# A two-layer hybrid decoder trunk: raw weight tiles in the common pool, the first weight ahead of x, low parts on DVE and token 0 ending alone

## The chip, the cores and the metric

The kernel runs on one core of a Trainium2 chip. The metric is the device time of one execution in microseconds (us); lower is better. The engines are PE (TensorE, matrix multiplication), DVE (VectorE), ACT (ScalarE), POOL (GpSimd) and SP (SyncE, which here only issues transfers).

## The reference

The input is `x`, 512 tokens by 1024 features, float32. Two layers follow one another; layer 0 mixes tokens by sliding-window attention, layer 1 by a chunked spatial gating unit (SGU):

```
for i in range(2):
    x += rmsnorm(mixer_i(rmsnorm(x)))        # mixer 0: attention, mixer 1: SGU
    x += rmsnorm(swiglu(rmsnorm(x)))         # the FFN, 2816 hidden features

attention: 16 query heads, 4 key/value heads of 64, rotary positions, window 128,
           a learned sink per head; softmax over 256 keys for each block of 128 queries
SGU:       z = gelu(h @ w_in); u, v = halves of z
           y = u * (tril(w_s) @ layernorm(v) + b_s); out = y @ w_out
swiglu:    (silu(h @ w_gate) * (h @ w_up)) @ w_down
```

All of it is float32.

## The kernel before, in words

Every float32 product is made of three matmuls. A tile is split into a high part (`hh` of activations, `wh` of weights) in a shorter type that PE multiplies at full rate, and the remainder (`hl`, `wl`); the product is high × high + high × low + low × high (`mm3`), summed in PSUM (`acc` tiles of 128 × 512). All of these matmuls have one line in the profile, L272.

Weights stream once through the core: 240 blocks of 128 × 1024 (512 KB), each a `raw` tile brought by a transfer issued on SP (L303). A block, or the sum of two for the FFN's product scheme, becomes one chunk: ACT writes the high part (`split`, L344), then DVE, or POOL for the first two chunks (`POOL_LOW`), subtracts it from raw to give the low part (L325 on DVE, L322 on POOL). `raw` tiles lie in a pool of their own of `NRAW` = 4, the split tiles, the tiles `xg` and the row constants in a pool `wp` of `NW` = 15. A transfer for a raw tile is issued when its slot is free; SP issues in the program's order.

The order of instructions on PE, DVE and ACT is the order in which Python emits them, and a planner sets it while it does. The main line emits matmuls and advances a clock of its own (`now`). Everything beside it (evacuations, norms, splits) is a `Side`, a generator with a due time; `tick()` runs whatever has come due between two matmuls, and when nothing is due, `split_idle()` may emit the next split, if two slots of `wp` are free. `until(f)` and `wait(t)` let time pass; as long as `now` is under `WARM`, they fill it with matmuls on a tile of zeros (`pass_time`, L240).

Stages follow in this order: projections q, k, v and attention (0 to about 180 us in the trace), the first FFN (to 548), the SGU, the second FFN. In attention a query block's probabilities are scaled (L1079 on DVE, L1083 on ACT), transposed by PE (`aux`, L1116), evacuated by ACT (`t`, L1120) and multiplied by v (PV, L1108: `acc<-t,vt`, four for a head pair). ACT and DVE then split the result into `ga` (L1130 high, L1135 low) for the output projection (`acc<-wh,ga`). The rotary step copies on ACT (L966, L976).

At the end of an FFN each token block (four of 128 tokens) has two halves of 512 features, which are 18 matmuls each; `ends` says in which order they are made. DVE adds a finished half to the block's sum `m` (L901), ACT sums squares (L476), DVE scales by the norm's row (L604), takes the reciprocal root in a chain of small steps on 128 × 1 values (L482 to L471, `rsqrt`), updates `x` (L617), and normalised x is transposed by PE (L554), from which `hh` (ACT, L567) and `hl` (DVE, L571) of the next stage come. The last token block of the second FFN ends in two quarters (L930) and the output x (L662).

At the start the tiles `xg` (x transposed, four tiles of 512 KB) become `hh` and `hl` with the norm's scales `c_cols` (L1390, L1393); `ORDER` says how these tiles and the first weight blocks follow one another on SP. Meanwhile `x` itself is read for the row sums of squares, whose reciprocal roots reach the query tiles through a small matmul (L1431).

Of the kernel before, what the change touches and what calls it, by code (L numbers as in the profile page):

```python
# [23 lines left out]
MAGIC = 0x5F3759DF  # L24
NW = 15
NP = 2
# [3 lines left out]
NT = 3  # L30
NRAW = 4
SETS = (8, 8)
# [5 lines left out]
DLAT = 1.7  # L38
X_0 = 4.0
RS = (0.27406385, -4.2420223, 5.2654107, -0.90349173, 1.7067959)  # L40
# [3 lines left out]
DIAG = (0, 1)  # L44
POOL_LOW = (0, 1)
ALT = (1, 2, 3)
WARM = 5.5
ORDER = (0, "w", 1, 2, "w", 3)
ACT_SQ = ()
# [100 lines left out]
def trunk_kernel(ctx, tc, x_t, xt, w, cols, rows, ws_t, consts, out):  # L150
# [6 lines left out]
    gp = pool("gp", 2)  # L157
    rawp = pool("rawp", NRAW)
    wp = pool("wp", NW)
# [7 lines left out]
    def nm(s):  # L167
        cnt[0] += 1
        return f"{s}_{cnt[0]}"
# [65 lines left out]
    def pass_time(t):  # L235
        if now[0] < WARM:
            if idle_ps[0] is None:
                idle_ps[0] = acc()
            while now[0] + 0.12 < min(t, WARM):
                nc.tensor.matmul(idle_ps[0][:, 0:256], zero[:, 0:P], zero[:], start=True, stop=True)  # L240
                now[0] += 0.214 if now[0] < 4.0 else 0.107
        now[0] = max(now[0], t)
# [42 lines left out]
    raws, chunks = {}, {}  # L285
    used, cur, hold, pace = [0], [0], [0.0], [5.1]
    left = [CB * u for _, _, u in STREAM]
    raw_used = [0]

    def fetch(free=0.0, most=NBLK):  # L290
        while len(raws) < min(NCH, most) and raw_used[0] + len(STREAM[len(raws)][0]) <= NRAW:
            c = len(raws)
            if c == NLATE:
                load_x()
# [6 lines left out]
            for b in reversed(STREAM[c][0]):  # L301
                raw = rawp.tile([P, CB * P], F32, tag="raw", name=nm("raw"))
                nc.sync.dma_start(raw[:], w[b])  # L303
                busy["d"] = max(busy["d"], now[0], free) + 1.46
                tiles.insert(0, raw)
# [3 lines left out]
    def split():  # L309
        c = len(chunks)  # L310
        fetch()
        tiles, ready = raws[c]
        raw = tiles[0]
        assert used[0] + 2 <= NW
        used[0] += 2
# [33 lines left out]
    def split_idle():  # L349
        c = len(chunks)  # L350
        if c >= NCH or used[0] + 2 + spare[0] > NW or (c and not chunks[c - 1][2].done):
            return False
# [9 lines left out]

    spare, stage = [0], [0]

    def chunk(i):
        c = i // CB
        while c >= len(chunks):
            until(lambda: not chunks or chunks[len(chunks) - 1][2].done)
            split()
        return c, chunks[c]  # L370
# [18 lines left out]

    def row_tile(o):  # L390
        used[0] += 1
        assert used[0] <= NW
        t = wp.tile([P, D], F32, tag="w", name=nm("row"))
        nc.sync.dma_start(t[:], rows[272 + o * D:272 + (o + 1) * D].partition_broadcast(P))
        return t
# [20 lines left out]
    xg = [wp.tile([P, 2, S], F32, tag="w", name=f"xg{q}") for q in range(NB)]  # L416
    used[0] += NB
    nc.gpsimd.dma_start(c_id[:], consts[:, 1280:1408])
    nc.gpsimd.dma_start(c_cols[:], cols)
    nc.gpsimd.dma_start(c_row[:], rows[0:272].partition_broadcast(P))  # L420
# [283 lines left out]
    def ffn(base, nx_in, g1o, nx_out):  # L704
# [188 lines left out]
        if 1:  # L893
            spare[0] = 0
            g1 = row_tile(g1o)
# [7 lines left out]

            ends = [(0, 0), (0, 1), (1, 0), (1, 1)]
            if nx_out is None:
                ends.pop()
            ends = [((0, 1), 0), ((0, 1), 1)] + [((2 + i,), c) for i, c in ends]
            for n, (ts, c) in enumerate(ends):
                if n == 2:
                    hold[0] = now[0] + 4 * BJ * 0.65  # L910
                for t in ts:
# [635 lines left out]
```

## Time and profile before

| what | value |
|---|---|
| runs | 1058.65, 1058.82, 1059.26 us; median 1058.82 |
| the profiled execution | 1059.33 us, of which the profile's span is 1057.5 |
| mean granted clock of PE | 0.989 |
| busy | PE 1031.1, weight load 854.7, DVE 684.7, ACT 469.6, POOL 23.8 us |
| matmuls | 5126 |
| moved from HBM | 135.69 MB, 130 GB/s over the span |

A row of the timeline is: start, duration, engine, line, operation, output <- inputs, size, count, and in brackets the engine's idle time before it and what ended that. A row of waits is: engine, what it was about to make, who ended the wait, us in total, how often, the longest. Span and run differ by what lies around the program.

### The profile page before, as it was taken

What the parts mean: (1) busy time and instruction counts of PE and PEld (TensorE: products, weight loads), DVE (VectorE), ACT (ScalarE), POOL (GpSimd) and SP (SyncE); (2) the same over time, 40 slices, a digit from 0 to 9 for tenths busy, and PEclk for the clock granted to TensorE, in tenths of its full rate; (3) what the DMA queues carried; (4) which work ended last, traced back from release to release, by engine and by line L of the source; (5) the groups of instructions that cost most, each with busy time, mean ns of one, the idle gap of its engine ahead of it and who ended that gap; (6) DMA issues with size and microseconds to landing.
All of it is one profiled execution on the core that took longest, in us unless ns stands there. A gap on an engine that the chain in (4) does not pass through costs nothing.

```text
span 1057.5 us, 13471 instructions
## 1 busy us (share of the span) xinstructions
PE 1031.1 (97%) x5126; PEld 854.7 (81%) x5126; DVE 684.7 (65%) x1276; ACT 469.6 (44%) x817; POOL 23.8 (2%) x22
## 2 busy tenths in 40 slices
PE   8998998999999999999989999999999999999996
PEld 7875665998888888888878888899888888888885
DVE  6798678743446566778495777474245666687736
ACT  5798666542233343435265343464224333334411
POOL 2000002000000000000010000010000000000000
PEclk9998999999999999999999999999999999999999
DMA  9422011343425644655431333133344553565402
GB/s 334 138 82 80 21 60 41 100 127 113 139 82 178 199 122 157 222 188 191 156 116 60 104 103 121 56 121 120 120 140 131 178 174 124 188 203 193 163 21 80
DMA packets 39057, 138.66 MB, mean 131 GB/s; under 512 B 4368, under 2 KB 4896, under 8 KB 38992
## 3 DMA queue, kind: packets, MB, share of 16 engines
q1 hardware_dynamic: 38304, 136.66, 39.3%
q8 instruction: 40, 0.66, 0.3%
q10 hardware_dynamic: 576, 0.92, 0.2%
q0 software_dynamic: 112, 0.23, 0.2%
q14 instruction: 25, 0.20, 0.1%
HBM read 135.69 MB, written 2.10 MB: 130 GB/s over the span
## 4 chain that ended last, share of the span: by engine, by line
PE 92%; DVE 3%; ACT 2%; issue 1%; DMA 0%; POOL 0%; DVEq 0%; ACTq 0%; POOLq 0%
PE acc L272 89%; PE acc L1108 1%; PE aux L1116 1%; PE aux L554 1%; ACT p L1070 1%; DMA c_cols<-cols 0%; ACT rt L966 0%; DVE wl L325 0%; DVE x L617 0%; DVE hl L1393 0%; ACT wh L344 0%; PE aux L552 0%; ACT t L1120 0%; DVE m L1210 0%; DVE rc L471 0%
## 5 line engine op out<-in xcount | busy, mean ns | idle before, releaser
L272 PE MATMUL acc<-hh,wh 128*128 128x512 f32 (+1 forms) x960 | 352.1, 367 | 0.0
L272 PE MATMUL acc<-hl,wh 128*128 128x512 f32 (+1 forms) x960 | 349.9, 364 | 0.0
L272 PE MATMUL acc<-hh,wl 128*128 128x512 f32 (+1 forms) x960 | 349.7, 364 | 0.0
L325 DVE TENSOR_TENSOR wl<-raw,wh 128x1024 fp32r<-128x1024 f32 x198 | 241.9, 1230 | 151.1 <-PE acc L272 78.2
L272 PEld LDWEIGHTS acc<-hh,wh 128*128 128x128 f32 x960 | 181.1, 189 | 29.4 <-issue 0.2
L272 PEld LDWEIGHTS acc<-hh,wl 128*128 128x128 f32 x960 | 181.1, 189 | 28.7
L272 PEld LDWEIGHTS acc<-hl,wh 128*128 128x128 f32 x960 | 181.1, 189 | 28.6 <-issue 0.2
L344 ACT ACTIVATE wh<-raw 128x1024 fp32r<-128x1024 f32 x160 | 165.6, 1052 | 55.0 <-PE acc L272 48.3
L272 PE MATMUL acc<-wh,rt 128*128 128x512 f32 x496 | 162.3, 389 | 0.0
L272 PE MATMUL acc<-wh,ga 128*128 128x512 f32 (+1 forms) x344 | 120.3, 399 | 3.6 <-DVE ga L1135 2.9
L272 PEld LDWEIGHTS acc<-wh,rt 128*128 128x128 f32 x496 | 93.1, 188 | 19.4
L272 PE MATMUL acc<-wl,rt 128*128 128x512 f32 x248 | 96.5, 389 | 0.0
L272 PEld LDWEIGHTS acc<-wh,ga 128*128 128x128 f32 x344 | 65.2, 191 | 21.1 <-DVE ga L1135 3.8
L853 DVE TENSOR_TENSOR m<-m,acc 128x512 f32<-128x512 f32 x80 | 51.8, 684 | 44.2 <-PE acc L272 33.0
L272 PE MATMUL acc<-wl,ga 128*128 128x512 f32 (+1 forms) x206 | 80.0, 388 | 0.0
L332 ACT ACTIVATE wh<-raw 128x1024 fp32r<-128x1024 f32 x40 | 42.3, 1059 | 71.0 <-DVE raw L337 71.0
L831 ACT ACTIVATE rt<-t 128x512 fp32r<-128x512 f32 x40 | 25.3, 633 | 87.1 <-DVE t L826 68.7
L740 ACT ACTIVATE t<-acc 128x512 f32<-128x512 f32 (+1 forms) x38 | 20.1, 529 | 95.0 <-PE acc L272 95.0
L272 PEld LDWEIGHTS acc<-wl,rt 128*128 128x128 f32 x248 | 46.6, 188 | 9.6
L337 DVE TENSOR_TENSOR raw<-raw,raw 128x1024 f32<-128x1024 f32 x40 | 48.8, 1219 | 0.0
L272 PEld LDWEIGHTS acc<-wl,ga 128*128 128x128 f32 x206 | 39.3, 191 | 6.6
L598 POOL TENSOR_TENSOR m<-m,row 128x512 f32<-128x512 f32 x12 | 16.8, 1407 | 1012.1 <-ACT acc L476 1012.1
(135 smaller groups left out, 990.5 us busy)
## 6 DMA issues: line engine op xcount, KB each, us to landing
raw<-w SPq DMA_DIRECT2D x240, 512.0 KB, 3.6
row<-rows SPq DMA_DIRECT2D x8, 512.0 KB, 5.2
xg<-xt SPq DMA_DIRECT2D x4, 512.0 KB, 7.1
x<-x_t SPq DMA_DIRECT2D x4, 512.0 KB, 11.9
out<-x SPq DMA_DIRECT2D x4, 256.0 KB, 2.1
out<-x ACTq DMA_DIRECT2D x3, 256.0 KB, 2.1
cs<-consts SPq DMA_DIRECT2D x1, 512.0 KB, 8.3
t<-ws_t SPq DMA_DIRECT2D x2, 256.0 KB, 5.9
```

Of the source, the lines that this page charges most:

```text
L272: nc.tensor.matmul(ps, a, b, start=start, stop=stop)
L325: nc.vector.tensor_tensor(wl[:], raw[:], wh[:].bitcast(F32), ALU.subtract)
L332: nc.scalar.activation(wh[:], raw[:], AF.Copy)
L337: nc.vector.tensor_tensor(raw[:], raw[:], tiles[1][:], op)
L344: nc.scalar.activation(wh[:], raw[:], AF.Copy)
L554: nc.tensor.transpose(dst, self.src[t][k // 4][:, (k % 4) * P:(k % 4 + 1) * P], ident)
L598: nc.gpsimd.tensor_tensor(self.m[c][:], self.m[c][:], self.g1[:, cols2[c]], ALU.mult)
L740: nc.scalar.activation(t1[:, hf], pg[:, hf], AF.Silu)
L831: nc.scalar.activation(hi, src, AF.Copy)
L853: nc.vector.tensor_tensor(d, d, ps[i][:], ALU.subtract if sign == "-" else ALU.add)
L1070: nc.scalar.activation(p(j), p(j), AF.Exp, bias=st[:, j:j + 1], accum_out=sm[:, j:j + 1])
L1108: nc.tensor.matmul(po[i * 64:i * 64 + 64, :], vt[n - nkt + 1 + kt][:, o:o + 64], todo[2 * kt + i], start=kt == 0, stop=kt == nkt - 1)
```

## The change

- `rawp` is gone. Raw tiles come from `wp`, which grows from 15 to 19 tiles; the planner counts `used + raw_used` against `NW`. At most 2 raw tiles may be outstanding, and 4 in stages 2 and 6, the gate and up products of the FFNs (`NRAW`). `room()` asks for a fetched block and two free slots before a split, and a row constant's tile waits for a slot.
- `ORDER`: the first weight block is fetched ahead of the first `xg`.
- `c_cols` is fetched by the first instruction of ACT's queue, not of POOL's; ACT runs a small activation on zeros right after it (`first_act`).
- `POOL_LOW` is empty: the first two low parts are made by DVE.
- `WARM` goes from 5.5 to 8.0, and a matmul on zeros counts 0.214 throughout: 37 instead of 26 of them.
- `ends`: of tokens 0 and 1 only the first halves are made together; token 0's second half now precedes token 1's. `hold` grows from 4 to 5 units.
- `X_0`, the planner's time for the first x tile, goes from 4.0 to 4.9.

```diff
-NW = 15
+NW = 19
-NRAW = 4
+NRAW = (2, 4)
-X_0 = 4.0
+X_0 = 4.9
-POOL_LOW = (0, 1)
+POOL_LOW = ()
-WARM = 5.5
-ORDER = (0, "w", 1, 2, "w", 3)
+WARM = 8.0
+ORDER = ("w", 0, 1, 2, "w", 3)
...
-    rawp = pool("rawp", NRAW)
...
-                now[0] += 0.214 if now[0] < 4.0 else 0.107
+                now[0] += 0.214
...
     def fetch(free=0.0, most=NBLK):
-        while len(raws) < min(NCH, most) and raw_used[0] + len(STREAM[len(raws)][0]) <= NRAW:
+        while len(raws) < min(NCH, most):
             c = len(raws)
+            n = len(STREAM[c][0])
+            if raw_used[0] + n > NRAW[stage[0] in (2, 6)] or used[0] + raw_used[0] + n > NW:
+                return
...
-                raw = rawp.tile([P, CB * P], F32, tag="raw", name=nm("raw"))
+                raw = wp.tile([P, CB * P], F32, tag="w", name=nm("raw"))
...
     def split():
         c = len(chunks)
-        fetch()
...
-        if c >= NCH or used[0] + 2 + spare[0] > NW or (c and not chunks[c - 1][2].done):
+        if c >= NCH or used[0] + raw_used[0] + 2 > NW or (c and not chunks[c - 1][2].done):
...
+    def room():
+        fetch()
+        return len(chunks) in raws and used[0] + raw_used[0] + 2 <= NW
 
     def chunk(i):
         c = i // CB
         while c >= len(chunks):
-            until(lambda: not chunks or chunks[len(chunks) - 1][2].done)
-            split()
+            until(lambda: c < len(chunks) or (not chunks or chunks[len(chunks) - 1][2].done) and room())
+            if c >= len(chunks):
+                split()
         return c, chunks[c]
...
     def row_tile(o):
+        until(lambda: used[0] + raw_used[0] < NW)
         used[0] += 1
...
+    nc.scalar.dma_start(c_cols[:], cols)
+    first_act = sp.tile([P, 8], F32, tag="first", name="first", bufs=1)
+    nc.vector.memset(first_act[:], 0.0)
+    nc.scalar.activation(first_act[:], first_act[:], AF.Copy)
     nc.gpsimd.dma_start(c_id[:], consts[:, 1280:1408])
-    nc.gpsimd.dma_start(c_cols[:], cols)
...
-            ends = [(0, 0), (0, 1), (1, 0), (1, 1)]
+            ends = [((0, 1), 0), ((0,), 1), ((1,), 1), ((2,), 0), ((2,), 1), ((3,), 0), ((3,), 1)]
             if nx_out is None:
                 ends.pop()
-            ends = [((0, 1), 0), ((0, 1), 1)] + [((2 + i,), c) for i, c in ends]
             for n, (ts, c) in enumerate(ends):
                 if n == 2:
-                    hold[0] = now[0] + 4 * BJ * 0.65
+                    hold[0] = now[0] + 5 * BJ * 0.65
```

Because the planner decides with these numbers, the order of instructions changes beyond the lines of the diff. Three places follow; the numbers behind an underscore tell tiles apart, and lines of the changed kernel stand a few higher than before.

On ACT at the program's start, before (`wh_183` is the first weight block, `hh` are the high parts of x):

```order
L1390 ACT_TABLE_LOAD
L1390 ACTIVATE hh_125<-xg_99,c_cols 128x512
L1390 ACTIVATE hh_126<-xg_99,c_cols 128x512
L344 ACTIVATE wh_183<-raw_107 128x1024
L1390 ACTIVATE hh_127<-xg_100,c_cols 128x512
L1390 ACTIVATE hh_128<-xg_100,c_cols 128x512
```

and now (L424 is the transfer of the scales, L427 the small activation, L346 the split, L1397 the high parts of x):

```order
L424 DMA c_cols<-cols 128x42
L427 ACT_TABLE_LOAD
L427 ACTIVATE first<-first 128x8
L346 ACTIVATE wh_169<-raw_106 128x1024
L1397 ACTIVATE hh_125<-xg_96,c_cols 128x512
L1397 ACTIVATE hh_126<-xg_96,c_cols 128x512
L1397 ACTIVATE hh_127<-xg_97,c_cols 128x512
```

The table load, the scales' transfer and the weight's high part have moved ahead of the first `hh`.

On ACT in the attention, about 148 to 153 us in the trace before (`t_1592` is the last of four transposed tiles that PE's PV needs, L476 a sum of squares, L344 a weight's split):

```order
L1120 ACTIVATE t_1572<-aux_1567 128x512
L1083 ACTIVATE p_1461<-p_1461,sm_1460 128x256
L1067 ACTIVATE es_1459<-es_1459 128x4
L1070 ACTIVATE p_1461,sm_1460<-p_1461,st_1458 128x256 x4
L476 ACTIVATE acc_1500,sq_1499<-m_1011 128x512
L344 ACTIVATE wh_1584<-raw_997 128x1024
L1120 ACTIVATE t_1592<-aux_1587 128x512
```

and now (`t_1591` is that tile, L485 the sum of squares):

```order
L1127 ACTIVATE t_1571<-aux_1566 128x512
L1090 ACTIVATE p_1468<-p_1468,sm_1467 128x256
L1074 ACTIVATE es_1466<-es_1466 128x4
L1077 ACTIVATE p_1468,sm_1467<-p_1468,st_1465 128x256 x4
L1127 ACTIVATE t_1591<-aux_1586 128x512
L485 ACTIVATE acc_1507,sq_1506<-m_966 128x512
L346 ACTIVATE wh_1598<-raw_1283 128x1024
```

The fourth `t` has moved ahead of the sum of squares and of the split. On PE, six matmuls of the output projection stand between the first two and the last two PV matmuls there, where before those four stood together with only a transpose between.

On DVE near the end of the attention, about 178 to 183 us (`ga_118` is the low part of the last attention output, L617 the update of x, L1210 an add to the output sum):

```order
L617 SCALAR_TENSOR_TENSOR x_91<-m_1013,rc_1826,x_91 128x512
L617 SCALAR_TENSOR_TENSOR x_91<-m_1014,rc_1826,x_91 128x512
L325 TENSOR_TENSOR wl_1838<-raw_1276,wh_1837 128x1024
L1210 TENSOR_TENSOR m_1016<-acc_1804,m_1016 128x512
L1135 TENSOR_TENSOR ga_118<-acc_1782,ga_117 128x4x128
```

and now:

```order
L626 SCALAR_TENSOR_TENSOR x_88<-m_968,rc_1849,x_88 128x512
L626 SCALAR_TENSOR_TENSOR x_88<-m_969,rc_1849,x_88 128x512
L327 TENSOR_TENSOR wl_1829<-raw_1643,wh_1828 128x1024
L1142 TENSOR_TENSOR ga_118<-acc_1781,ga_117 128x4x128
L1217 TENSOR_TENSOR m_971<-acc_1832,m_971 128x512
```

`ga_118` has moved ahead of the add; on PE six matmuls that do not need it now stand between the last PV and its first use, where before there was none.

At the end of the first FFN, on PE, the transposes of tokens 0 and 1 came before six matmuls of token 3's last half and the first of the next stage; now 18 matmuls of token 3's last half stand between the third group of transposes and the first matmul of the next stage.

More of the change, by code (lines that the diff above doesn't have):

```diff
@@ L286, in trunk_kernel @@
     used, cur, hold, pace = [0], [0], [0.0], [5.1]
+    stage = [0]
     left = [CB * u for _, _, u in STREAM]
@@ L310, in split @@
         c = len(chunks)
-        fetch()
         tiles, ready = raws[c]
         raw = tiles[0]
-        assert used[0] + 2 <= NW
+        assert used[0] + raw_used[0] + 2 <= NW
         used[0] += 2
@@ L361, in split_idle @@
         return True
-    spare, stage = [0], [0]
+    def room():
+        fetch()
+        return len(chunks) in raws and used[0] + raw_used[0] + 2 <= NW
     def chunk(i):
@@ L390, in row_tile @@
     def row_tile(o):
+        until(lambda: used[0] + raw_used[0] < NW)
         used[0] += 1
-        assert used[0] <= NW
         t = wp.tile([P, D], F32, tag="w", name=nm("row"))
@@ L893, in ffn @@
         if 1:
-            spare[0] = 0
             g1 = row_tile(g1o)
```

## The prediction

> **What bounds the kernel now.** I read the busy shares first, then the list of TensorE's (PE's) waits, then the granted clock around those waits.
>
> ```profile
> span 1057.5 us, 13471 instructions
> PE 1031.1 (97%) x5126; PEld 854.7 (81%) x5126; DVE 684.7 (65%) x1276; ACT 469.6 (44%) x817; POOL 23.8 (2%) x22
> ```
>
> ```profile
> PE acc L1108 <- ACT t L1120: 6.6, 3, 3.8
> PE acc L272 <- ACT wh L344: 3.1, 1, 3.1
> PE acc L272 <- DVE ga L1135: 2.9, 2, 2.6
> PE acc L272 <- DVE hl L571: 2.7, 1, 2.7
> ...
> PE acc L272 <- DVE hl L1393: 0.8, 1, 0.8
> PE acc L272 <- ACT ga L1130: 0.7, 1, 0.7
> ```
>
> PE is idle for 1057.5 − 1031.1 = 26.4 us. The six waits (us in total, times, longest) hold 16.8 of them; most of the rest is the tail after the last matmul. Since the matmuls stay as they are, the change can win only idle PE time and time at a lower clock:
>
> ```profile
> 9.00:13.00 4.00, 3.47 (x17) 3.47 (x18) 3.23 (x3) 3.88 (x6) 2.42 (x2) 0.57 1.03 420
> 98.00:106.00 8.00, 6.51 (x29) 4.04 (x30) 4.91 (x15) 4.34 (x9) 0.00 (x0) 0.57 0.22 66
> 152.00:157.00 5.00, 5.00 (x26) 3.70 (x25) 3.82 (x13) 1.34 (x3) 0.00 (x0) 0.66 0.32 105
> 182.00:188.00 6.00, 5.11 (x20) 4.20 (x21) 5.81 (x29) 1.71 (x4) 1.28 (x1) 0.72 0.30 94
> 551.00:557.00 6.00, 5.93 (x20) 4.64 (x21) 5.91 (x10) 1.78 (x3) 0.00 (x0) 0.72 0.79 251
> 557.00:1049.00 492.00, 492.00 (x2440) 418.34 (x2440) 302.98 (x505) 191.47 (x289) 8.48 (x6) 1.00 0.39 126
> ```
>
> Columns: stretch, its length, busy time of PE, weight load, DVE, ACT and POOL, then the granted clock (third number from the right). The last row is the steady state: PE full, clock 1.00, nothing to win. After each long wait the clock is lower: (1 − 0.66) × 5 = 1.7 us of PE time lost at 152, and likewise 1.7 at 182 and 1.7 at 551, 1.7 at 9 and 3.4 at 98 (of which 0.7 falls into the wait itself, so 2.7). So a wait of 2.6 us costs about 4.3.
>
> **The start** (one term for ORDER, c_cols, the early activation, POOL_LOW and WARM).
>
> ```profile
> 1.06 5.39 PE L240 MATMUL acc<-zero 128*128 128x256 bf16 x26 [1.06 <-DVE zero L232]
> 1.94 5.24 DMA c_cols<-cols
> 4.84 1.28 ACT L1390 ACT_TABLE_LOAD   x1 [4.84 <-DMA xg<-xt]
> 7.20 1.33 ACT L1390 ACTIVATE hh<-xg,c_cols 128x512 fp32r<-128x512 f32 x2 [1.07 <-DMA c_cols<-cols]
> 9.53 0.58 PE L272 MATMUL acc<-wh,hh 128*128 128x256 f32 x1 [3.08 <-ACT wh L344]
> 12.96 2.45 POOL L322 TENSOR_TENSOR wl<-raw,wh 128x1024 fp32r<-128x1024 f32 x1 [1.02 <-ACT wh L344]
> 13.04 1.34 ACT L1390 ACTIVATE hh<-xg,c_cols 128x512 fp32r<-128x512 f32 x2 [0.16 <-DMA xg<-xt]
> 13.07 2.89 DVE hl L1393
> 16.01 0.39 PE L272 MATMUL acc<-wh,hl 128*128 128x256 f32 x1 [0.84 <-DVE hl L1393]
> 19.83 0.88 PE L272 MATMUL acc<-wl,hh 128*128 128x256 f32 x6
> L325 DVE TENSOR_TENSOR wl<-raw,wh 128x1024 fp32r<-128x1024 f32 x198 | 241.9, 1230 | 151.1 <-PE acc L272 78.2
> ```
>
> Before, c_cols holds the first hh until 7.2, the first weight follows on ACT, and PE starts at 9.53 with the clock gone. Then the low part hl of the third x tile takes 2.89 us while POOL runs a low part beside it; 31 more matmuls of 0.12 us lead from 16.01 to the low pass near 19.7. After: with the first weight ahead of xg, the first xg lands one 512 KB transfer after 4.84 (some 1.3 us, so 6.1), ACT has split the weight by then, and its table is loaded before any data is there. PE starts at about 7 to 7.6, when the warm-ups end: at 5.39 / 26 = 0.207 us the 37 of them would reach 8.7, somewhat less once the clock rises; a start as late as 8.7 still does not bind, because the fourth xg, which stays the sixth transfer, does. Its hh starts at 13.04 and takes 1.34. DVE, without POOL beside it, has one new low part of 1.23 before the first hl and one before the fourth pair; hl at 0.7 each follows hh at 0.7 distance: 13.04 + 1.34 + 0.7 ≈ 15.2. The last eight matmuls follow, so the low pass starts at about 16.3: gain 3.4. Bounds: 2 (if DVE stretches again by about 1.4) and 4. What hides the two low parts (2.5 us of DVE) is its wait for hh; if that cover is gone, hl is late by up to 1.2, inside the bound. The row statistics end at 23.9 as before and are next needed after 18 instead of 15 matmuls of the first query tile, at about 24.1 by the new clock: this just fits.
>
> **The attention stalls** (a consequence of the shared pool, its planner conditions and NW: splits are issued earlier or later, and with them the order on ACT and DVE).
>
> ```profile
> 60.00:98.00 38.00, 35.42 (x196) 25.20 (x194) 36.56 (x107) 36.65 (x86) 0.00 (x0) 1.00 0.25 84
> 95.51 2.91 ACT L966 ACTIVATE rt<-rt,c_cols 32x512 f32<-32x512 f32 x4
> 99.49 1.97 PE L1108 MATMUL acc<-t,vt 128*64 128x512 f32 x2 [3.78 <-ACT t L1120]
> 149.61 0.58 ACT L476 ACTIVATE acc<-m 128x512 f32<-128x512 f32 x1
> ...
> 150.22 1.04 ACT L344 ACTIVATE wh<-raw 128x1024 fp32r<-128x1024 f32 x1
> ...
> 151.80 1.07 PE L1108 MATMUL acc<-t,vt 128*64 128x512 f32 x2 [2.58 <-ACT t L1120]
> ...
> 180.42 1.21 DVE L325 TENSOR_TENSOR wl<-raw,wh 128x1024 fp32r<-128x1024 f32 x1
> 182.89 0.76 PE L272 MATMUL acc<-wh,ga 128*128 128x512 f32 x2 [2.60 <-DVE ga L1135]
> ```
>
> At 99.49 ACT itself is full (36.65 of 38 us): between two evacuations t it runs 5.2 us before and 4.4 us in the new order (2.91 of rotary copies, 0.95 weight, 0.54 copy). The stall shrinks from 3.78 to about 3.2 and the lower clock most likely stays: gain 0.5 (−2 to 4, the upper end if the clock holds).
>
> At 151.80 the awaited t stood behind a row sum (0.61) and a weight split (0.95); now it stands ahead of both, and six output matmuls (1.4 us) lie between the first two and the last two probability matmuls. 2.58 − 0.61 − 0.95 − 1.4 is below zero; I leave 0.6 for the matmuls that are missing as cover where they stood, and 0.7 for three transposes now in a row: gain 2.58 + 1.7 − 1.3 = 3.0 (0 to 4.3).
>
> At 182.89 the awaited ga stood behind two x updates, a weight's low part and an add; now it stands ahead of the add (0.6), and six matmuls (1.4) follow the last probability matmul. The chain that remains, split 0.95, low part 1.21 and ga 0.6, is 2.8 from the probability matmuls' start, and PE has 0.9 + 1.4 + 0.5 = 2.8 of work: a remainder of about 1 with both waits there, and the clock stays up. Gain 0.69 + 2.60 + 1.7 − 1.0 = 4.0, of which I take 3.5.
>
> A row that speaks against counting all this: the granted clock falls at 98, 152.7, 183.4 and 552, some time after a wait begins and even with work running. The Trainium skill, "TensorE: Matmul & The Clock Gate", Part 1, says that activity is judged in a free-running window of about 3.4 us and the clock halves after an idle one. Taken strictly, waits of 2.6 us would cost no clock, and the sum would be 5.1 smaller; the trace disagrees, since 1.7 us of clock were lost after each. That the windows run freely agrees: what is left of a wait can fall whole into one window or be shared between two.
>
> **The seam from the first FFN to the gating unit, and the tail** (ends and hold).
>
> ```profile
> 546.18 0.14 DVE L482 SCALAR_TENSOR_TENSOR u<-sq 128x1 f32<-128x1 f32 x1
> ...
> 547.47 1.41 DVE L617 SCALAR_TENSOR_TENSOR x<-m,rc,x 128x512 f32<-128x512 f32 x2
> 548.80 0.68 DVE L901 TENSOR_TENSOR m<-acc,m 128x512 f32<-128x512 f32 x1
> ...
> 550.54 0.87 DVE L571 SCALAR_TENSOR_TENSOR hl<-aux,c_cols,hh 128x256 fp32r<-128x256 f32 x2
> ...
> 551.07 0.50 PE L272 MATMUL acc<-wh,hl 128*128 128x512 f32 x1 [2.68 <-DVE hl L571]
> ...
> 1050.08 0.75 DVE L930 TENSOR_TENSOR m<-acc,m 128x256 f32<-128x256 f32 x2
> ```
>
> Before, tokens 0 and 1 end together, and 2.68 us of PE time go by until their second hl pair, behind x update, add and weight on DVE. Now token 0 ends a half (18 matmuls of 0.23 = 4.1 us) earlier. From the end of token 2's first half DVE needs add 0.7, hl 0.9, the small chain 1.3 (546.18 to 547.47), x 1.4, weight 1.2, add 0.7, hl 0.9 = 7.1, while PE has 42 matmuls and four transpose groups (9.6 + 1.4 = 11.0); at the third pair it is 11.9 against 13.7. So nothing is late: gain 2.68 + 1.7 = 4.4 (2 to 4.4; the third pair is next, by 1.8). In the tail x of token 2 and the add of the last token's first quarter are done before PE's last matmul (1049.6), not after it: DVE starts the last add at 1049.65, ACT's square follows, and the small chain starts at about 1050.8, while before two adds and two scalings (0.75 a pair) from 1050.08 on put it near 1051.7: gain 0.9 (0.3 to 1.3).
>
> **The shared raw tiles themselves.** Weight transfers now wait for slots that PE frees, and they are issued in order on SP. By the program's order each transfer's slot is free at least 13 us of PE time before its first use, and 24 in the FFNs. From issue to use it needs its landing plus 1.0 (ACT) plus 1.2 (DVE), so I cost it at nothing:
>
> ```profile
> raw<-w SPq DMA_DIRECT2D x240, 512.0 KB, 3.6
> ```
>
> **Sum.** 3.4 + 0.5 + 3.0 + 3.5 + 4.4 + 0.9 = 15.7. The order is new throughout the attention, where ACT and DVE are nearly full, so I give one new short wait with its lost clock back, 1.7. The profiled execution took 1059.33 (span plus 1.83; 0.5 above the median, 1058.82): 1059.33 − 14.0 = 1045.3.
>
> **Rivals.**
> 1. The attention stalls form again elsewhere: 96% of ACT in that stretch leaves no room, and only the order moves. Against it: the waits at 152 and 183 stand behind single instructions that have moved. Then start, seam and tail remain, 3.4 + 4.4 + 0.9 = 8.7, and one more stall of 2.6 + 1.7 may take half of that back: 1050.6 to 1055.
> 2. Slower: raw tiles in the shared pool. Outside the gate and up stages two transfers may be outstanding, and SP issues in order, so one that waits for PE holds those behind it. A use takes 1057 / 240 = 4.4 us a block and the way from slot to weight 3.6 + 1.0 + 1.2 = 5.8: a transfer let go only one block ahead stalls PE by 1.4, with 1.7 of clock each time 3.1. Five such blocks undo the gain, seven give 1067. The leads of 13 us speak against it.
> 3. The stalls fall across two windows: the clock holds at 99 too, 2.7 more: 1042.6. The Trainium skill, "TensorE: Matmul & The Clock Gate", Part 1, would have it so for a wait under 3.4 us.
> 4. The change does little: the low parts on DVE delay hl as POOL did, and the seam's chain is late at its third pair: start 1, tail 0.9, and the attention as in rival 1: about 1057.5, within what a measurement of this kernel can tell from no change, 0.2% or 2.1 us.
>
> **How the numbers follow.** Forecast (1044 to 1050) 0.61, rival 1 0.18, rival 2 0.09, rival 3 0.07, rival 4 0.05. Leaving out rival 2, rival 4 and a piece of rival 1 gives 1041.5 to 1055. Faster by over 0.2% holds the forecast, rivals 1 and 3: 0.86; same 0.05; slower 0.09.
>
> **What would show it.** PE's first real matmul before 8.8, the low pass at 16 to 17, clock 1.00 through 9 to 13; no wait over 1.5 us and clock 1.00 near 148 and 180; a wait of about 3 us still near 95; no wait at the seam near 535 to 550; the small chain within 1.3 us of the last matmul. Wrong would be: new waits of PE on L344's or L325's successors with a raw transfer behind them (rival 2), or waits on t and ga of 2 us or more at other places (rival 1).

## The result and the profile after

The changed kernel takes 1044.27 us (median of 4 runs, 1044.11 to 1044.54) against 1059.04 for the kernel before in the same session (1058.65 to 1059.56): the ratio is 0.986, 95% interval 0.9843 to 0.9878. 1045.3 was forecast, 1041.5 to 1055. The profiled execution took 1044.54, its span is 1042.8.

The head of the profile after, and its list of PE's waits:

```profile
span 1042.8 us, 13516 instructions
PE 1026.1 (98%) x5137; PEld 851.5 (82%) x5137; DVE 683.0 (65%) x1279; ACT 470.9 (45%) x818; POOL 18.5 (2%) x19
```

```profile
PE acc L1115 <- ACT t L1127: 3.9, 1, 3.9
PE acc L271 <- DVE ga L1142: 3.9, 2, 2.7
...
PE acc L271 <- DVE hl L1400: 0.4, 1, 0.4
...
```

PE's idle time falls from 26.4 to 1042.8 − 1026.1 = 16.7 us. Its busy time falls by 5.0 although there are 11 more matmuls on zeros; this is the clock. Two waits of over 2 us are left. Neither is near 148, where the wait at 152 stood before (first row), nor at the seam (second row). The columns are those of the prediction, PE's busy time first and the clock third from the right:

```profile
144.00:152.00 8.00, 7.75 (x52) 4.42 (x53) 4.87 (x18) 7.48 (x22) 0.00 (x0) 1.00 0.00 0
530.00:548.00 18.00, 18.00 (x89) 14.93 (x88) 16.29 (x41) 14.36 (x30) 1.29 (x1) 1.00 0.57 205
```

Since most matmuls keep their place in PE's order, the start of the same matmul in both traces tells where the time went. This table is worked out from the timelines' PE rows:

| place | before | after | lead | gained since the row above |
|---|---|---|---|---|
| first weight's low pass (`wl,hh`) | 19.83 | 16.91 | 2.92 | 2.9 |
| before the second half of the attention | 137.45 | 134.97 | 2.48 | −0.4 |
| between the places of the waits at 152 and 183 | 167.18 | 160.80 | 6.37 | 3.9 |
| in the first FFN | 199.43 | 190.31 | 9.12 | 2.7 |
| in the SGU | 576.39 | 562.59 | 13.80 | 4.7 |
| last matmul | 1049.30 | 1035.57 | 13.73 | −0.1 |
| end of the span | 1057.5 | 1042.8 | 14.7 | 1.0 |

The rows of the timeline after that stand behind it, in order of time:

```profile
7.89 0.36 PE L271 MATMUL acc<-wh,hh 128*128 128x256 f32 x1
10.92 0.39 PE L271 MATMUL acc<-wh,hl 128*128 128x256 f32 x1 [0.40 <-DVE hl L1400]
11.86 1.06 ACT L346 ACTIVATE wh<-raw 128x1024 fp32r<-128x1024 f32 x1
12.97 0.39 PE L271 MATMUL acc<-wh,hh 128*128 128x256 f32 x1
14.09 1.41 DVE L1400 SCALAR_TENSOR_TENSOR hl<-xg,c_cols,hh 128x512 fp32r<-128x512 f32 x2
16.91 4.00 PE L271 MATMUL acc<-wl,hh 128*128 128x256 f32 x32
...
86.41 0.51 PE L271 MATMUL acc<-wh,ga 128*128 128x512 f32 x1 [1.21 <-DVE ga L1142]
...
97.08 1.97 PE L1115 MATMUL acc<-t,vt 128*64 128x512 f32 x2 [3.95 <-ACT t L1127]
...
149.75 0.66 PE L1123 MATMUL aux<-c_id,p 128*128 128x128 f32 x4 [0.25 <-ACT t L1127]
...
173.79 0.89 PE L271 MATMUL acc<-wh,ga 128*128 128x512 f32 x2 [2.67 <-DVE ga L1142]
...
1036.94 0.16 DVE L491 SCALAR_TENSOR_TENSOR u<-sq 128x1 f32<-128x1 f32 x1 [0.18 <-ACT acc L658]
```

The wait at 152 is gone but for 0.25, the one at 99 is as long as it was (3.95 at 97.08), the one at 183 is 2.67 at 173.79, and there is a new one of 1.21 at 86.41. The last small chain starts 1.37 after the last matmul, before it was 1051.68 − 1049.30 = 2.38.

The clock can be read more sharply than the prediction did. It takes two values, 1.00 and 0.50, and the time between two changes is always a multiple of 3.413 us. These are the stretches at half speed of the kernel before, then those of the kernel after (columns as in the prediction, the clock third from the right):

```profile
9.38:12.79 3.41, 3.26 (x15) 3.26 (x16) 2.66 (x2) 3.41 (x6) 2.37 (x1) 0.50 1.03 420
98.13:104.95 6.82, 5.46 (x23) 3.34 (x24) 3.89 (x12) 3.17 (x7) 0.00 (x0) 0.50 0.25 77
152.74:156.15 3.41, 3.41 (x20) 2.94 (x19) 2.30 (x9) 1.20 (x2) 0.00 (x0) 0.50 0.47 153
183.46:186.87 3.41, 3.41 (x10) 2.63 (x9) 3.41 (x16) 0.48 (x1) 0.89 (x1) 0.50 0.25 103
552.10:555.51 3.41, 3.41 (x10) 2.64 (x9) 3.41 (x7) 1.78 (x3) 0.00 (x0) 0.50 0.80 268
```

```profile
95.70:102.53 6.83, 5.45 (x23) 3.38 (x24) 4.89 (x14) 3.84 (x8) 0.00 (x0) 0.50 0.00 0
170.80:174.21 3.41, 0.74 (x4) 0.38 (x3) 3.41 (x4) 0.88 (x4) 1.25 (x1) 1.00 0.31 114
174.21:177.62 3.41, 3.41 (x10) 2.64 (x9) 3.39 (x20) 1.67 (x3) 1.30 (x1) 0.50 0.32 89
```

I call one such step of 3.413 us a window. Up to the last matmul, six half-speed windows have become three, each worth up to 3.41 / 2 = 1.7 us of PE's time: about 5 us less busy time beside the 9.7 us less idle time. The row 170.80:174.21 points at the cause: PE worked 0.74 of 3.41 us in it, and the window after it runs at half speed. An experiment below tests this.

### The profile page after: what moved, and what is told of

It is laid out like the page before. It is cut to its first block, busy times and chain, and to the rows that moved or that the text cites. A ratio compares the mean times of both kernels' runs of the same rounds, so it can differ in the third digit from the quotient of the medians.

```text
span 1042.8 us, 13516 instructions
## 1 busy us (share of the span) xinstructions
PE 1026.1 (98%) x5137; PEld 851.5 (82%) x5137; DVE 683.0 (65%) x1279; ACT 470.9 (45%) x818; POOL 18.5 (2%) x19
## 4 chain that ended last, share of the span: by engine, by line
PE 93%; ACT 3%; DVE 3%; DMA 1%; issue 0%; SPq 0%; DVEq 0%; ACTq 0%
PE acc L271 90%; ACT p L1077 1%; PE aux L563 1%; DMA xg<-xt 1%; PE acc L1115 1%; ACT rt L973 1%; PE aux L1123 1%; DVE p L1055 0%; DVE wl L327 0%; DVE p L1086 0%; ACT t L1127 0%; PE aux L561 0%; ACT wh L346 0%; ACT p L1090 0%; DVE m L1217 0%
## 5 line engine op out<-in xcount | busy, mean ns | idle before, releaser
L327 DVE TENSOR_TENSOR wl<-raw,wh 128x1024 fp32r<-128x1024 f32 x200 | 244.8, 1231 | 145.7 <-ACT wh L346 77.7
L346 ACT ACTIVATE wh<-raw 128x1024 fp32r<-128x1024 f32 x160 | 165.9, 1052 | 87.3 <-PE acc L271 57.6
L485 ACT ACTIVATE acc<-m 128x512 f32<-128x512 f32 x30 | 18.0, 599 | 38.4 <-DVE m L909 34.0
```

The lines of the kernel that those rows point to most:

```text
L327: nc.vector.tensor_tensor(wl[:], raw[:], wh[:].bitcast(F32), ALU.subtract)
L346: nc.scalar.activation(wh[:], raw[:], AF.Copy)
L485: nc.scalar.activation(junk, src, AF.Square, accum_out=s[:, c:c + 1])
```

## The experiments

A difference is given against the runs of the kernel before in the same session; the changed kernel itself stands at −14.8 in that measure.

**The three parts alone.** The kernel before with the start's lines only:

```diff
+X_0 = 4.9
+POOL_LOW = ()
+WARM = 8.0
+ORDER = ("w", 0, 1, 2, "w", 3)
...
+    nc.scalar.dma_start(c_cols[:], cols)
...
+    nc.scalar.activation(first_act[:], first_act[:], AF.Copy)
```

> The kernel before with the start's part alone (ORDER, c_cols on ACT's queue, the early activation, POOL_LOW empty, WARM, X_0). Theory (each part is worth what its own place in the trace shows): the low pass starts near 16.9 instead of 19.8, 2.9 us won; the waits near 151 and 183 and at the seam (2.6 to 2.7 us each, with the clock's 1.7) stay, so about 1056. Rival (the parts work only together, since the planner orders the attention by its own clock, which the start moves): anything from 1051 to 1061, with other waits than those of before.

Measured: 1054.26 (1052.92 to 1055.65) against 1058.49, ratio 0.9957 [0.9943, 0.9972], so −4.2. The low pass starts at 16.92, as in the whole change. These lines also move the planner's order in the attention: the wait at 99 breaks up, and one of 2.08 for `ga` forms at 87.32.

With the lines on `ends` and `hold` only:

```diff
+            ends = [((0, 1), 0), ((0,), 1), ((1,), 1), ((2,), 0), ((2,), 1), ((3,), 0), ((3,), 1)]
...
+                    hold[0] = now[0] + 5 * BJ * 0.65
```

> The kernel before with the end order of the FFNs and hold alone. Theory: no wait of PE at the seam (2.68 + 1.7 won) and the tail 1.0 shorter, so 5.4 won: about 1053.6, all waits of the attention as before. Rival (the seam is free because weights are split earlier from the shared pool): the wait at the seam stays at 2 us or more and only the tail's 1.0 is won, 1058.

Measured: 1053.74 (1052.83 to 1054.10), ratio 0.9951 [0.9936, 0.9966], so −4.75. No wait is left at the seam, and the attention's waits are those of before.

With the shared pool and the planner's conditions only:

```diff
+NW = 19
+NRAW = (2, 4)
...
+                raw = wp.tile([P, CB * P], F32, tag="w", name=nm("raw"))
```

> The kernel before with the shared pool, NW, NRAW and the planner's conditions alone. Theory: what start and ends do not explain, 14.8 - 2.9 - 5.4 = 6.5 us, comes from here, in the attention: 1052.5, with the wait near 151 gone; the seam's wait stays. Rival (the pool by itself costs, because SP's transfers wait for PE): 1059 or more, with waits for weights behind raw transfers.

Measured: 1049.95, ratio 0.9915 [0.9901, 0.993], so −8.5, with a wide spread of 1047.93 to 1051.50. The wait near 152 is gone here too, but for 0.25. The profile is of the fastest of the four runs; these are its timeline and its windows around 172:

```profile
172.14 0.73 PE L271 MATMUL acc<-wh,ga 128*128 128x512 f32 x2 [2.68 <-DVE ga L1140]
...
167.44:170.85 3.41, 2.02 (x8) 1.34 (x8) 3.26 (x5) 2.53 (x7) 1.62 (x1) 1.00 0.47 154
170.85:174.26 3.41, 2.12 (x9) 1.78 (x10) 3.41 (x15) 1.54 (x3) 0.74 (x1) 1.00 0.00 0
174.26:177.68 3.42, 3.28 (x21) 2.64 (x21) 3.35 (x12) 1.11 (x4) 0.56 (x1) 1.00 0.84 266
```

A wait as long as the change's (2.68 us) is shared by two windows here, 41% and 38% idle, and the clock stays up. The slowest run had a mean granted clock of 0.988 against 0.994 in this one; which windows it lost, no profile shows. The parts sum to 17.5 where the whole brings 14.8. They need not add up, since the start and the pool each move the planner's order in the attention, and since what a wait costs depends on how it falls into the windows.

**Idle time as the cause of the lost clock.** The changed kernel with 32 matmuls on a constant (result unused) inside the PV pair at 97, and 22 ahead of the last output group, where the wait for `ga` was. No other instruction moves.

```diff
+        def fill(n):
+            if n:
+                d, z = aux(), c_id[:].bitcast(mybir.dt.bfloat16)
+                for _ in range(n):
+                    nc.tensor.matmul(d[:, 0:256], z[:, 0:P], z, start=True, stop=True)
...
+                    if (pr, n, kt, i) == (0, 1, 1, 1):
+                        fill(32)
...
+                    fill(22)
```

> The changed kernel with matmuls on constants put into the two waits of PE that are left: 32 inside the probability pair that waits 3.95 us at 97, 22 ahead of the last output group that waits 2.67 us at 173.8; everything else stands in the same order. Theory (the lower clock after a wait comes from PE being idle in it): the waits remain about as long, but the clock stays at 1.00, and 2.8 + 1.2 = 4.0 us are won: 1040.3. Rival (the clock falls for another reason than idleness, or such matmuls do not count): 1044.3. A second rival (they delay the matmuls behind them): up to 1047.

Measured: 1041.83 (1041.72 to 1041.97), ratio 0.984 [0.9824, 0.9857], so −16.7, about 2 better than the change. No half-speed window is left between the warm-up and the last matmul, and the runs lie within 0.25. Work without use takes the place of the waits, and the time falls: the lost clock is due to PE's idleness. It falls by less than expected; part of this is a wait for DVE's next product that comes up behind the one filled:

```profile
171.14 0.73 PE L271 MATMUL acc<-wh,ga 128*128 128x512 f32 x2 [0.24 <-DVE ga L1150]
179.52 0.39 PE L271 MATMUL acc<-hl,wh 128*128 128x256 f32 x1 [0.80 <-DVE hl L580]
```

**The order of weight splits near 174.** The planner's numbers for the output stage let the splits come later; the last entry, `(1,)` for `(1, 2)`, also moves the third token tile's products from POOL to DVE:

```diff
-PLAN = [..., (6.0, 0.8, 0.0, (3,), (1, 2)), ...
+PLAN = [..., (4.0, 0.8, 1.2, (3,), (1,)), ...
```

> The changed kernel with the planner's row for the second half of the attention set to (4.0, 0.8, 1.2, (3,), (1,)): splits are less urgent there and keep away from chains, and token 2's scaling goes from POOL to DVE. On DVE the last output low part ga now stands ahead of token 1's x update and of a weight's low part instead of behind both. Theory (the wait of 2.67 us at 173.8 is DVE's order plus POOL's scaling, which stretches the low part from 1.22 to 2.29): the wait goes, with its clock: 2.67 + 1.2 = 3.9 won, 1040.4; at least 2 of it if a short wait forms at the first transposes of the FFN. Rival (DVE is simply full there, and any order waits): a wait of 2 us or more comes back within 10 us, 1043 to 1046.

Measured: 1048.16 (1047.85 to 1048.72), ratio 0.9899 [0.9884, 0.9914], about 4 slower than the change. The wait for `ga` is gone and a longer one stands 10 us on:

```profile
183.55 0.58 PE L271 MATMUL acc<-hl,wh 128*128 128x256 f32 x1 [4.41 <-DVE hl L580]
```

DVE is busy for 11.81 of the 12 us from 172 to 184: it has more to do there than PE's work covers, and here another order only moved the wait. Since the run also puts two products more on DVE, it does not test the order by itself.

**The scales' queue and the early activation.** The changed kernel with these two undone:

```diff
-    nc.scalar.dma_start(c_cols[:], cols)
-    first_act = sp.tile([P, 8], F32, tag="first", name="first", bufs=1)
-    nc.vector.memset(first_act[:], 0.0)
-    nc.scalar.activation(first_act[:], first_act[:], AF.Copy)
+    nc.gpsimd.dma_start(c_cols[:], cols)
```

> The changed kernel with c_cols again on POOL's queue and without the early activation; the first weight still goes ahead of x, and the low parts stay on DVE. Theory (from the second x tile on, which lands at 9.3, the start is paced by the transfers and the second weight's split at 12.9): the first hh starts at about 7.2 instead of 6.4, PE's first real matmul at 8.6 instead of 7.9, and the low pass still near 17.0: 0 to 0.2 us slower, 1044.3 to 1044.5. Rival (these two are what gave the start's 2.9): 1046 to 1047.

Measured: 1044.00 (1043.34 to 1044.57), ratio 0.9861 [0.9844, 0.9877]: no difference. The low pass starts at 16.85. In this profile the wait for `ga` is the same, and again it lies across two windows and costs no clock:

```profile
172.88 0.74 PE L271 MATMUL acc<-wh,ga 128*128 128x512 f32 x2 [2.66 <-DVE ga L1139]
...
168.42:171.84 3.42, 1.79 (x8) 1.13 (x6) 3.31 (x4) 2.35 (x7) 1.61 (x1) 1.00 0.52 153
171.84:175.25 3.41, 2.38 (x10) 1.97 (x11) 3.41 (x15) 1.68 (x3) 1.00 (x1) 1.00 0.09 13
```

**Raw tiles in the gate and up stages.** Two instead of four outstanding:

```diff
-NRAW = (2, 4)
+NRAW = (2, 2)
```

> The changed kernel with NRAW = (2, 2): in the gate and up stages too only two raw tiles may be outstanding, which is one chunk there, since two blocks make one. Theory of the slower rival (a transfer let go only one chunk ahead comes late): each of the 40 such chunks waits for landing 3.5, add 1.2, high part 1.05 and low part 1.2 = 7.0 us after the add freed the slots, against 24 matmuls of 0.39 = 9.4 us of PE per chunk: still hidden, so within 1 us of 1044.3 but with the waits of ACT and DVE for raw transfers grown from nothing to several us each. If transfers of a pair queue behind one another by 2 us or more, PE waits in every chunk: 1060 and over.

Measured: 1115.60 (1115.04 to 1116.16), ratio 1.0535 [1.0514, 1.0556], about 71 slower than the change, where the theory had it within 1. The list of PE's waits is headed by splits:

```profile
PE acc L271 <- ACT wh L334: 23.5, 20, 3.1
PE acc L271 <- DVE wl L327: 17.0, 24, 0.8
```

So too few slots do cost what the prediction's rival 2 feared, and the change's own numbers stay on the safe side of it. The way there is not shown. Where a chunk is the sum of two blocks, two slots let no transfer run ahead; but the list of waits has only 4.1 us of ACT on raw transfers and none of DVE, so it may as well be that the planner issues sums and splits late, since `room()` asks for a fetched block first.

**Why the wait for `ga` stayed.** Ahead of `ga`, some of DVE's instructions take far longer than elsewhere, and each time POOL multiplies by the norm's row. In the kernel before it was the pair of x updates, 2.43 where such a pair takes 1.42 at 173.71:

```profile
178.07 2.43 DVE L617 SCALAR_TENSOR_TENSOR x<-m,rc,x 128x512 f32<-128x512 f32 x2
178.43 1.52 POOL L598 TENSOR_TENSOR m<-m,row 128x512 f32<-128x512 f32 x1 [4.77 <-ACT acc L476]
```

In the changed kernel it is a scaling of p (POOL's first product runs from 161.20 to 162.48), a small step and the low part:

```profile
160.67 1.96 DVE L1086 TENSOR_SCALAR p<-p,sm 128x256 f32<-128x256 f32 x3
167.05 1.30 POOL L607 TENSOR_TENSOR m<-m,row 128x512 f32<-128x512 f32 x1 [4.57 <-ACT acc L485]
167.43 0.94 DVE L491 SCALAR_TENSOR_TENSOR u<-sq 128x1 f32<-128x1 f32 x1
170.44 1.61 POOL L607 TENSOR_TENSOR m<-m,row 128x512 f32<-128x512 f32 x1 [2.09 <-ACT acc L485]
170.84 2.29 DVE L327 TENSOR_TENSOR wl<-raw,wh 128x1024 fp32r<-128x1024 f32 x1
```

L491 ends at 168.37, as POOL's product ends at 168.35; the low part ends at 173.13, which is 172.05, POOL's end, plus 1.08. This looks as if DVE stood still until POOL is through. The test cuts POOL's products to 8 of 512 columns, so that the output is no longer the same, and moves no instruction:

```diff
-                nc.gpsimd.tensor_tensor(self.m[c][:], self.m[c][:], self.g1[:, cols2[c]], ALU.mult)
+                w = slice(0, 8 if stage[0] == 1 else S)
+                nc.gpsimd.tensor_tensor(self.m[c][:, w], self.m[c][:, w], self.g1[:, cols2[c]][:, w], ALU.mult)
```

> The changed kernel, but in the first attention's output stage POOL's products m*row (L607) work on 8 of 512 columns only, so the output differs there; no instruction moves on any engine. It tests why the wait for ga near 174 stayed (2.67). Theory: POOL's product of 1.6 us stands beside DVE's low part and doubles it (2.29 instead of 1.22), and the one before holds DVE's first small step (0.94 instead of 0.15): 1.07 + 0.79 = 1.9 of the wait. Then the low part takes 1.22, the wait at 174 shrinks to about 0.8, the small steps of 0.94 and 1.33 take 0.15 and 0.21, and the time falls by 1.9, and by up to 1.7 more if the clock holds there: 1040.7 to 1042.4. Rival: DVE's list ahead of ga is too long by itself: the wait stays above 2 us and the time within 0.5 of the changed kernel's 1044.3.

Measured: 1039.99 (1039.82 to 1040.59), ratio 0.9823 [0.9809, 0.9838], so −18.6, 3.9 better than the change and a little below the range expected.

```profile
159.69 0.88 DVE L1087 TENSOR_SCALAR p<-p,sm 128x256 f32<-128x256 f32 x3
...
168.53 1.22 DVE L327 TENSOR_TENSOR wl<-raw,wh 128x1024 fp32r<-128x1024 f32 x1
...
170.41 0.73 PE L271 MATMUL acc<-wh,ga 128*128 128x512 f32 x2 [0.27 <-DVE ga L1143]
```

The low part takes 1.22 again, the small step 0.15 and the scalings of p 0.88. The wait shrinks from 2.67 to 0.27, and no window from 102 to the last matmul runs at half speed. POOL, busy for 2% of the span, was worth 2.4 us of waiting and a half-speed window.

**The low parts at the start.** The changed kernel with the first two back on POOL:

```diff
-POOL_LOW = ()
+POOL_LOW = (0, 1)
```

> The changed kernel with POOL_LOW back at (0, 1): the low parts of the first two weight chunks on POOL instead of DVE, all else in place. Theory as in the prediction: POOL's low parts stretch DVE's hl beside them (2.89 for one group before), so the low pass starts 0.7 to 1.4 later than 16.9, and the time is 1045.0 to 1045.7. Rival: the low pass is paced by the second weight's split on ACT, done at 12.9, and 32 matmuls follow it without a gap, so DVE's hl has room: the low pass stays within 0.3 of 16.9, and the time within 0.4 of 1044.3.

Measured: 1044.95 (1044.30 to 1045.47), ratio 0.9869 [0.9854, 0.9884], so −13.7: 1.1 slower than the change, which the intervals do not separate. The trace does separate them:

```profile
6.03 2.35 POOL L324 TENSOR_TENSOR wl<-raw,wh 128x1024 fp32r<-128x1024 f32 x1 [3.33 <-ACT wh L346]
7.06 2.53 DVE L1400 SCALAR_TENSOR_TENSOR hl<-xg,c_cols,hh 128x512 fp32r<-128x512 f32 x2 [6.04 <-ACT hh L1397]
...
13.79 2.71 DVE L1400 SCALAR_TENSOR_TENSOR hl<-xg,c_cols,hh 128x512 fp32r<-128x512 f32 x2 [1.05 <-ACT hh L1397]
...
17.79 0.40 PE L271 MATMUL acc<-wl,hh 128*128 128x256 f32 x2
```

Two pairs of `hl` take 2.5 to 2.7 beside POOL instead of 1.41, and the low pass starts at 17.79, 0.9 later. The profiled execution itself took 1044.30, no longer than the change's, because its waits fell otherwise into the windows: up to the last matmul one window runs at half speed, not three.

**The wait at 97 as a matter of order.** A higher cost for one tile's rotary copies makes ACT issue them ahead of the evacuations `t`:

```diff
-                    f = A(n, f, 0.14)
+                    f = A(n, f, 0.22 if (pr, j) == (1, 0) else 0.14)
```

> The changed kernel, but the planner's fixed cost for one rotary copy on ACT is 0.22 instead of 0.14 for one tile (first of the second pair). ACT then issues the four rotary copies (2.9 us) ahead of the probability evacuations t, and between two evacuations t there stand at most a weight split or one row group. It tests whether the wait of 3.95 near 97 is a matter of order. Theory: it is; the 2.9 us no longer stand between two t, the longest wait for t is under 1.5, and the clock stays at 0.9 or more near 96 to 104 (0.61 in the window of the changed kernel): 1.5 to 4 us faster, 1040.3 to 1042.8. Rival: ACT is full (96% of its time here), so PE waits as long somewhere else between 84 and 104, in one piece or in two: the waits there sum to 4 to 5 us again and the time is within 1 of 1044.3.

Measured: 1043.32 (1043.20 to 1043.66), ratio 0.9854 [0.9837, 0.987], so −15.3, 0.5 better than the change, which the intervals do not separate.

```profile
87.94 1.22 PE L271 MATMUL acc<-wh,ga 128*128 128x512 f32 x2 [2.46 <-DVE ga L1142]
...
97.16 1.07 PE L1115 MATMUL acc<-t,vt 128*64 128x512 f32 x2 [0.88 <-ACT t L1127]
...
84.13:87.54 3.41, 1.35 (x14) 0.78 (x12) 3.27 (x13) 3.35 (x9) 0.00 (x0) 1.00 0.14 24
87.54:90.95 3.41, 3.02 (x7) 2.37 (x8) 3.34 (x13) 3.36 (x11) 0.00 (x0) 0.50 0.35 137
```

The theory fell. The wait for `t` shrinks to 0.88, the one for `ga` at 86 doubles to 2.46, and one half-speed window stands behind it, where the change has two behind its wait at 97. PE's waits from 84 to 102 sum to 4.2 against 5.2, as the rival had it. ACT is busy for 13.48 of the 13.65 us ahead of 95.70 in the changed kernel, and for 13.45 of the 13.65 ahead of 94.37 here: it is full, so a wait has to be somewhere.

The same order with 22 matmuls of fill ahead of the last output group:

```diff
...
+                    fill(22)
```

> The order of the run with the moved rotary copies, and 22 matmuls on a constant ahead of the last output group of the first attention, as in the run with dummy matmuls (2.6 us of PE work in place of the wait near 174, so that the clock stays up). Theory: the fill is worth about 1.2 here, half of what the two fills brought together (2.4), on top of the order's 1.5 to 4: 1039 to 1041.6. Rival: if the order alone brings nothing, 1042.5 to 1043.5.

Measured: 1043.26 (1043.10 to 1043.87), ratio 0.9854 [0.984, 0.9869]: the fill adds nothing to this order. It holds the clock at 174, but in its profile PE idles 54% of the window ahead of 87.35 and 18% of the half-speed one from 87.35, and two windows go there instead of one. It is a miss of the theory, and why the second window was lost only in this kernel's profile I cannot show; the windows lie 0.2 us otherwise against the program (87.35 here, 87.55 there).

**The products on DVE.** To the kernel with both fills, the output stage's products of the third token tile go from POOL to DVE:

```diff
-PLAN = [..., (6.0, 0.8, 0.0, (3,), (1, 2)), ...
+PLAN = [..., (6.0, 0.8, 0.0, (3,), (1,)), ...
```

> The kernel with the two groups of dummy matmuls (1041.83), and in the first attention's output stage the third token tile's two products m*row move from POOL to DVE; the order of PE is the same, DVE gets two products of 0.68, one of them just ahead of the awaited ga. Theory: POOL's product holds DVE longer than the product itself takes: DVE pays 2 x 0.68 and saves 1.07 (the low part of 2.30 takes 1.22) and 1.1 (the small step of 1.33 takes 0.24). The waits near 171 (0.24) and 180 (0.80) go, and the time falls by 0.5 to 1.0: 1040.8 to 1041.4. Rival: a product in line on DVE must wait for ACT's square of the same tile, and what DVE then waits stands ahead of ga: the wait near 171 grows by 0.5 or more, and the time is 1041.8 or above.

Measured: 1040.69 (1040.62 to 1040.81, 5 runs), ratio 0.9828 [0.9815, 0.9842], so −18.6, just below the range expected. This is the fastest kernel here that leaves no work out: 3.8 better than the change, and 1.9 better than the fills alone (1.1 by the medians).

```profile
165.01 0.94 DVE L491 SCALAR_TENSOR_TENSOR u<-sq 128x1 f32<-128x1 f32 x1
168.43 1.22 DVE L327 TENSOR_TENSOR wl<-raw,wh 128x1024 fp32r<-128x1024 f32 x1
169.56 0.69 DVE L613 TENSOR_TENSOR m<-m,row 128x512 f32<-128x512 f32 x1
```

DVE takes on 0.69 and is spared 1.07 in the same place. The wait for `ga` near 171 goes, and the one of 0.80 for `hl` shrinks to 0.50. L491 is still held for 0.94, since the second tile's products stay on POOL.

## Why the prediction was right, point by point

Its time was 1.0 above the measured median, and its sum of 14.0 stands against 14.7 in the spans. The terms were less exact than the sum. Three brought 2.0 more in all than forecast and two 1.3 less, so part of the closeness is luck:

| term | predicted | measured | what the runs showed |
|---|---|---|---|
| start | 3.4 | 2.9 | paced by PE's own work and the second weight's split |
| wait at 99, and the new wait | 0.5 − 1.7 | −0.4 | the old one stayed, the new one cost no clock |
| wait at 152 | 3.0 | 3.9 | gone entirely |
| wait at 183 | 3.5 | 2.7 | 2.67 of waiting and its window stayed |
| seam | 4.4 | 4.7 | as worked out |
| tail | 0.9 | 0.9 | as worked out (1.0 behind the last matmul, −0.1 ahead of it) |

**Start.** The low pass came at 16.9 instead of 16.3. The step that failed is "the fourth xg binds": PE ran 32 matmuls of 0.12 without a gap from 12.97 to 16.91, and 12.97 is just behind the end of ACT's split of the second weight (11.86 + 1.06 = 12.92). The split held PE for only 0.17, since the matmul before it started at 12.68 and they follow at 0.12; from 10.92 on PE had hardly another gap. So what failed is the count of what is left behind the last `hl`: when the prediction had it ready, at 15.2 (its own terms give 15.1), PE still had 14 matmuls ahead of the low pass, not eight. The cover for the two low parts on DVE held; with POOL's parts back, 0.9 of the 2.9 is lost. Moving the scales and the activation brings nothing to the time, as the run without them shows. The other 2.0 lies in the weight ahead of x, WARM and X_0, which no run takes apart. The Trainium skill, "DMA: Bandwidth & Descriptors", "Issuing engines are not separate DMA queues", says that starting transfers on several engines saves only the time that it takes to start them. The time agrees (1044.00 without the move), the trace only in part: from ACT's queue `c_cols` was issued 1.2 us earlier (0.74 against 1.94 in the kernel before) and also landed sooner after that, 4.3 us against 5.2.

**Wait at 99.** It was expected to shrink to 3.2 and did not. That the whole of this stretch goes by ACT's total, as rival 1 had it, fits this place: every new order here (the start alone, the pool alone, the moved rotary copies) has waits that sum to 3.3 to 4.2 us between 84 and 102, where the kernel before has 4.1 and the change 5.2. Rival 3 did not come true either: the clock is at half speed for two windows in and behind the wait, as before. A new short wait was foreseen and came (1.21), but with 28% idle in its window it cost no clock, so the 1.7 given back was 1.2. That the row reads −0.4 and not −1.4 is owed to 0.7 us less busy time of PE for the same 612 matmuls and 0.2 us in small gaps, which I cannot assign.

**Wait at 152.** The evacuation ahead of the row sum and the split, together with the six matmuls of cover, was enough; no run tells the two apart. The 0.6 and 0.7 that I kept back for missing cover did not show, but for 0.25.

**Wait at 183.** Here the mechanism failed: a remainder of about 1 with the clock up was forecast, and 2.67 with a half-speed window behind it came. The remaining chain was put at 2.8 (split, low part 1.21, `ga`); the low part took 2.29, the small step ahead of the x update 0.94 instead of 0.15, and the scalings of p 1.96 instead of 0.88, all held by POOL. The run with short products gives these 2.9 back and 2.4 of the wait; 0.45 of the rest is a wait of DVE for PE that it has instead. That the term still gained 2.7 comes from the waits of 0.35, 0.55 and 0.69 that went, and from 1.2 us less busy time for the same 158 matmuls, which I cannot assign: that this term came near its 3.5 is luck. The prediction had written of POOL stretching DVE at the start, and had not looked for it here, though the pair of x updates of 2.43 stands in the trace of the kernel before, just ahead of the low part that it read. The Trainium skill, "SBUF — State Buffer", "🔬 SBUF: two separate sides", has DVE and GpSimd on one shared port pair, held as an exclusive lock for a whole instruction; a step of 0.15 that ends as POOL's product ends, and a low part that has 1.08 of its 1.22 still to run at that point, agree with it.

**Seam and tail** went as worked out, and the half-speed window behind the seam went with its wait.

**The shared raw tiles** cost nothing, as predicted: no listed wait of PE is on a split. With two slots in the gate and up stages they cost about 71 us, so a loss such as rival 2 feared was a matter of one number.

**The clock.** I had set the Trainium skill's rule of an idle window against the trace, and had said that strictly taken it would leave waits of 2.6 us without cost. The traces show a third thing. Over the 14 profiles of this case there are, counted from their PE rows up to the last matmul, 36 full-speed windows with at least 50% of PE's time idle that are followed by a half-speed window, and one with 49%; 64 with 15 to 49% are not followed by one. The one exception, 57%, is in a warm-up; of the windows that hold the last matmul, one with 54% kept the clock too. So about half a window is enough here, and a wait of 2.6 us costs up to 1.7 more if over 1.7 of it falls into one window, and nothing if it is shared. The Trainium skill, "TensorE: Matmul & The Clock Gate", Part 1, gives the window as free-running and 3413 ns long, with which the stretches agree.

## What to carry to other kernels

Where PE is nearly full, cut waits to under 1.7 us before you try to remove them: a wait of up to that length, alone in its window, cost only itself here, a longer one up to half a window of 3.4 us more. Useless matmuls in a wait can be worth their place. Before moving a two-input operation to POOL to relieve DVE, look at which DVE instructions run beside it: products of 1.3 to 1.6 us off the critical path held the instructions on which PE waited. Where ACT or DVE was busy for 98% of 12 us or more, a new order moved the wait; at 152, where ACT was busy for 75% of the 12 us ahead, a new order removed it. In a full stretch, take work off the engine.

## What the runs showed of the hardware

- The granted clock has only the values 1.00 and 0.50 here, and it changes on a grid of 3.413 us; the windows of 552.10 and 183.46 lie 108 × 3.413 apart. The grid's place against the program differs between runs (170.80:174.21 after, 168.42:171.84 with the scales moved back). Runs of one program can then differ by up to 1.7 us a wait: the runs of the shared pool alone spread over 3.6 us with mean granted clocks of 0.988 to 0.994, those with both waits filled over 0.25.
- In a half-speed window far less idle time was enough to stay there: 9 windows with 17% or more were followed by another, and one with 16% was not.
- DVE instructions with two tensor inputs wait for the end of POOL's product: 0.94 for a step of 0.15, 2.29 for a low part of 1.22. So does the scaling of p, which has one tensor input: three take 1.96 beside POOL's product of 1.28, and 0.88 beside one cut to 8 columns. POOL is held likewise: in this stage its product takes 1.28 to 1.30, and 1.61 where DVE's x update was running when it started.
